# One transformer trunk on one core: all 2 KB tiles of SBUF at one place modulo 256, and another order of work at the start

## The chip, the core and the metric

The kernel runs on one core of one Trainium2 chip. The metric is the device time of one execution in microseconds (us); the time of the kernel before is the median of three runs. Differences under 0.2% (3.8 us here) can hardly be told from none.

TensorE (PE) multiplies matrices: a *stationary* tile of 128 by 128 is loaded (a row named PEld), and a *moving* tile of up to 512 columns is streamed past it. VectorE (DVE), ScalarE (ACT) and GpSimd (POOL) do the elementwise work, and SyncE (SP) issues the transfers from HBM to the on-chip memory SBUF, which has 128 partitions. A tile lies at one address in all partitions; "place modulo 512" is that address, in bytes, modulo 512.

## What is computed

Two layers on a sequence of 256 rows of 1024 numbers, all in float32. Cut to what matters here:

```
cond = silu(c)
for l in range(2):
    sh1, sc1, g1, sh2, sc2, g2 = split(cond @ w_ada[l] + b_ada[l], 6)
    h = rms_norm(x) * (1 + sc1) + sh1
    x = x + g1 * token_mixer(h, ... w_in[l], ..., w_branch_a/b/c[l], w_out[l])
    h = rms_norm(x) * (1 + sc2) + sh2
    f = swiglu(h, ffn_w_gate, ffn_w_up, ffn_w_down) if l == 0 else moe_ffn(h, router, 8 experts, top 2)
    x = x + g2 * f
return rms_norm(x, final_norm_w)
```

## The kernel before

Every weight comes from HBM once, in pieces of 1 MB (128 partitions of 8 KB, the tile `raw`), issued by SP as soon as a `raw` buffer is free. To keep float32 accuracy on TensorE each piece is split into a high part and the rest: ACT writes `whi` (L170) and DVE writes `wlo = raw - whi` (L172), and the activations are split in the same way (`hh` and `hl`, `ah` and `al`, `xx`, `act`, `yh` and `yl`). A product is then three matmuls, which `mm3` issues: high by high, high by low, low by high. All are recorded at L96, so that they are told apart by their tiles. In the rows a matmul reads as `out<-moving,stationary`, whichever operand is named first: where both are listed, the weights `whi` and `wlo` are the moving operand for `hh`, `hl`, `ah`, `al`, `act`, `xx`, `yh`, `yl`, and in the convolutions of the mixer (256 columns) it is the other way round.

The stages follow one another: the start (`start`, layer 0's modulation, its normalised input `x`, and the first four column blocks of `w_in`), the mixer of layer 0, the dense feed-forward block, the mixer of layer 1, and the mixture of experts (`moe`), which takes from 870 us to the end. In `moe` each expert multiplies its gathered rows `xx` (128 rows, 8 stationary tiles for the high and 8 for the low part, written by `gather`) with 28 pieces of gate and up weights, in 7 blocks of 4 pieces. A piece is 4 x 3 matmuls of 512 columns, a block 48 of them, and between two blocks stand the 4 transposes of the block before (L1566). Then 14 pieces of down weights are multiplied with `act`, 168 matmuls. There are 8 experts, so 56 blocks.

The order in the start is made by the order of the code and by a scheduler, which may move an instruction ahead of others on its engine. In a step `k` of the 8 steps there, DVE reduces two columns of the modulation (L199), ACT applies them to `xT` (L353), writes `hh` (L354) and the high parts of the weights (L347), and DVE writes the low parts (L357) and `hl` (L355). A group of matmuls on a high part alone (`warm`, 8 of them) keeps TensorE at work before the first step.

Tiles come from pools which lie one behind the other in SBUF, so that the place of every tile follows from the sizes of those ahead of it in its pool and in the pools before.

Of the kernel before, what the change touches and what calls it, by code (L numbers as in the profile page):

```python
# [10 lines left out]
F32 = mybir.dt.float32  # L11
# [3 lines left out]
AF = mybir.ActivationFunctionType  # L15
# [4 lines left out]
P = 128  # L20
D = 1024
S = 256
NT = S // P
# [38 lines left out]
def trunk_kernel(ctx, tc, a, out, dbg=None):  # L62
# [5 lines left out]
    wp = ctx.enter_context(tc.tile_pool(name="wp", bufs=2))  # L68
    pp = ctx.enter_context(tc.tile_pool(name="pp", bufs=2, space=PSUM))

    ones = cp.tile([P, P], F32, name="ones")
    V.memset(ones, 1.0)
    xs = cp.tile([P, NT, D], F32, name="xs")
# [1 line left out]
    pv = [cp.tile([P, NPP], F32, name=f"pv{l}") for l in range(DEPTH)]  # L75
    pos = cp.tile([P, NT], I32, name="pos")
    rt = cp.tile([P, KD, NE], F32, name="rt")
    ident = cst[:, C_ID:C_ID + P]
    U = cst[:, C_U:C_U + P]
    mask = cst[:, C_MASK:C_MASK + P]  # L80
# [24 lines left out]
    def small(w, name, dt=F32, bufs=2):  # L105
        return cp.tile([P, w], dt, name=name, tag=name, bufs=bufs)
# [38 lines left out]
    def load_raw(src, k, n, raw=None):  # L145

        raw = raw_tile() if raw is None else raw
        last["load"] = nc.sync.dma_start(raw[:, :k * n], src)
        return raw
# [161 lines left out]
    def start(tile, puts, ready):  # L311


        crow = [tile("crow") for _ in range(2)]
        for c in range(2):
            nc.sync.dma_start(crow[c][0:1, :], a["c"][:, c * 512:(c + 1) * 512])
        loads()
        for c in range(2):
            ps = smtile()
            mm(ps, ones[0:1, :], crow[c][0:1, :], True, True)  # L320
            A.activation(sc_b[:, c * 512:(c + 1) * 512], ps, AF.Silu)
        bias = pv[0][:, PP_BADA:PP_BADA + 48].rearrange("p (a b n) -> p a b n", a=2, b=3)[:, :, 1]
        V.tensor_scalar(bias, bias, 1.0, None, op0=OP.add)
        xn = [[tile("xn") for _ in range(2)] for _ in range(NT)]
        rs = start_scales(lambda t, c: xn[t][c])
        for t in range(NT):
            A.activation(xn[t][0], xs[:, t, :512], AF.Copy, scale=rs[t])
            V.tensor_scalar(xn[t][1], xs[:, t, 512:], rs[t], None, op0=OP.mult)
        xT = [tile("xT") for _ in range(4)]
        for i in range(4):  # L330
            ps = trtile()
            for j in range(2):
                for t in range(NT):
                    k = 2 * i + j
                    T.transpose(ps[:, j * S + t * P:j * S + (t + 1) * P], xn[t][k // 4][:, k % 4 * P:(k % 4 + 1) * P], ident)
            if i % 2:
                V.tensor_copy(xT[i], ps)
            else:
                A.activation(xT[i], ps, AF.Copy)
        acc = {}  # L340
        for k in range(KD):
            ra = load_raw(a["w_ada_pair"][0, 0, k], 1, 2 * D)
            rw = load_raw(a["w_first"][k], 1, 1872)
            parts = []
            for o, n in ((0, 848), (848, 1024)):
                hi, lo = ring()
                A.activation(hi[:, :n], rw[:, o:o + n], AF.Copy)  # L347
                parts.append((hi, lo, o, n))
            if k == 0:
                warm(parts[0][0], WARM)  # L350
            run(ada_cols(0, k, KD, ra))
            x = xT[k // 2][:, k % 2 * S:(k % 2 + 1) * S]
            A.activation(x, x, AF.Identity, scale=modc[0][:, 8 + k:9 + k], bias=modc[0][:, k:k + 1])  # L353
            last["copy"] = A.activation(hh[:, k], x, AF.Copy)  # L354
            last["sub"] = V.tensor_sub(hl[:, k], x, hh[:, k].bitcast(F32))  # L355
            for hi, lo, o, n in parts:
                V.tensor_sub(lo[:, :n], rw[:, o:o + n], hi[:, :n].bitcast(F32))  # L357
            if not acc:
                acc.update({(0, 0): mmtile(), (0, 1): mmtile(), (1, 0): mmtile(), (1, 1): mmtile(), (2, 0): smtile(),
                            (2, 1): smtile(), (3, 0): smtile(), (3, 1): sstile()})  # L360
            for first, (l_, r_) in enumerate(((hh, 0), (hl, 0), (hh, 1))):
                for t in range(NT):
                    for i, (c0, n) in enumerate(FIRST):
                        w = parts[i // 2]
                        mm(acc[i, t][:, :n], l_[:, k, t * P:(t + 1) * P], w[r_][:, c0 - w[2]:c0 - w[2] + n],
                           k == 0 and first == 0, k == KD - 1 and first == 2)
        ready()
        for i, (c0, n) in enumerate(FIRST):
            for t in range(NT):
                puts[i](t, acc[i, t][:, :n])  # L370
# [55 lines left out]
    def run(gen):  # L426
        for _ in gen:
            pass
# [104 lines left out]
    def mixer(l, after=None):  # L533

        with tc.tile_pool(name=f"mx{l}", bufs=1, reuse_waits="tile") as mp, \
                tc.tile_pool(name=f"mb{l}", bufs=1, reuse_waits="tile", side="right") as bp, \
                tc.tile_pool(name=f"mc{l}", bufs=1, reuse_waits="tile", side="right") as qp:

            def wg(name, dt=F32):
                return mp.tile([P, 512], dt, name=name, tag="w2k", bufs=16)  # L540
# [769 lines left out]
    def moe(l):  # L1310
        with tc.tile_pool(name=f"mw{l}", bufs=1, reuse_waits="tile", side="right") as xp, \
# [11 lines left out]
            sel = mp.tile([P, NT, NE], F32, name="sel")  # L1323
            ovi = mp.tile([P, 4], I32, name="ovi")
            ovs = mp.tile([P, 3, 2, NT], F32, name="ovs")
            with tc.tile_pool(name=f"mr{l}", bufs=1, reuse_waits="tile") as rp, \
                    tc.tile_pool(name=f"me{l}", bufs=1, reuse_waits="tile") as ep:
                rest, weights = route(l, rp, h2, slot, wsel, sel)
                pair = lambda e: choose(mp, [lambda t, i=i: slot[:, t, i:i + 1] for i in (e, e + 1)])
                Pm = pair(0)  # L1330
                behind("Pm", rest)
                ready = [(x, Pm, i) for i, x in enumerate(gather(l, ep, h2, Pm, 2, True))]
                behind("xl", weights)
                late = {16: 2, 17: 3, 27: 3}
                ahead.extend(load_raw(first_srcs[i], 4, 512, shot(xp, late[i], "raw") if i in late else None)
                             for i in range(15, 28))
                row_tile[l, 5] = lambda: mp.tile([P, 512], F32, name="g2", tag="g2", bufs=2)
                ada_rows(l, 5)
                g2 = [rows[l, 10 + c] for c in range(2)]

                def after_first(c):
                    if c == 1:
                        with tc.issue_after(last["act"].ins), tc.issue_after(last["tr"].ins):
                            overflow_data(ep, slot, wsel, sel, ovi, ovs)
                def finish():

                    fw, o, f = (raw_tile() for _ in range(3))
                    nc.sync.dma_start(fw[:, :D], a["final_w"])
                    o, f = (x.rearrange("p (t n) -> p t n", t=NT) for x in (o, f))
                    for t in range(NT):  # L1350
                        rs = rms_scale(t, lambda c: o[:, t, c * 512:(c + 1) * 512])
                        for c in range(2):
                            cs = slice(c * 512, (c + 1) * 512)
                            G.tensor_mul(f[:, t, cs], xs[:, t, cs], fw[:, cs])
                        for c in range(2):
                            cs = slice(c * 512, (c + 1) * 512)
                            if c:
                                V.tensor_scalar(o[:, t, cs], f[:, t, cs], rs, None, op0=OP.mult)
                            else:
                                A.activation(o[:, t, cs], f[:, t, cs], AF.Copy, scale=rs)  # L1360
                            nc.sync.dma_start(out[t * P:(t + 1) * P, cs], o[:, t, cs])

                for e in range(NE):
                    x, Pm, i = ready.pop(0)

                    def between():
                        Pm = behind("lo", pair, e + 1)
                        ready.extend((x, Pm, i) for i, x in enumerate(gather(l, ep, h2, Pm, 2)))
                    expert(l, e, ep, xp, x, lambda t, Pm=Pm, i=i: Pm[:, t, i], lambda t, e=e: wsel[:, t, e:e + 1], g2,
                           after_first if e == 0 else None, between if e % 2 and e < NE - 1 else None)  # L1370
                stages.flush()
                finish()
                overflow(l, mp, ep, xp, h2, g2, ovi, ovs, finish)
# [281 lines left out]
        for _ in range(n):  # L1655
            mm(ps, x[:, :P], x[:, :512], True, True)

    WARM = 8

    def late_loads():  # L1660
        with tc.issue_after(last["load"].ins):
# [5 lines left out]
            nc.sync.dma_start(rt.rearrange("p k n -> p (k n)"), a["moe_router"][0, 0, 0])  # L1667

    def loads():
        for t in range(NT):  # L1670
            nc.sync.dma_start(xs[:, t], a["x"][t * P:(t + 1) * P])
        nc.sync.dma_start(cst[:, :C_U], a["consts"][:, :C_U])
        nc.sync.dma_start(pv[0], a["params"][0])

# [121 lines left out]
```

## Time and profile before

| | |
|---|---|
| median of 3 runs | 1892.44 us (1891.72 to 1893.65) |
| the profiled execution | 1891.01 us, of which the span from first to last instruction is 1889.2 us |
| PE busy | 97% of the span, 9490 matmuls |
| DVE busy | 85% |
| ACT busy | 65% |
| HBM read | 527.41 MB, 280 GB/s over the span |
| chain that ended last | PE 87%, DVE 6%, ACT 3% |

The profile is of one execution. A matmul's row has its start and a duration that overlaps the next one, so the distance from one start to the next, here called a step, says how fast TensorE goes, and the duration does not. The chain that ended last is followed back from the last instruction, at each point to what released it. Its pieces of TensorE run from the first start of a group to the next group, so that a piece of n matmuls divided by n is the mean step.

### The profile page before, as it was taken

How to read it: one execution, taken by the hardware profiler on the slowest of the kernel's cores; microseconds unless marked ns; L12 is line 12 of the kernel's file. 1: busy time of each engine (PE TensorE's matmuls, PEld its weight loads, DVE VectorE, ACT ScalarE, POOL GpSimd, SP SyncE). 2: the span in 40 equal slices, each digit the busy share in tenths (PEclk: the TensorE clock that was granted, in tenths of full speed). 3: DMA queues.
4: the chain of work that ended last, by engine and by line, in shares of the span. 5: the costliest groups of instructions: out<-in, count | busy, mean ns of one | idle time of the engine just before them, and what ended most of it. 6: DMA issues, size and time to landing. Idle time of an engine off the chain costs nothing.

```text
span 1889.2 us, 25651 instructions
## 1 busy us (share of the span) xinstructions
PE 1841.5 (97%) x9490; PEld 1545.4 (82%) x9490; DVE 1602.2 (85%) x2313; ACT 1231.6 (65%) x1599; POOL 43.3 (2%) x61
## 2 busy tenths in 40 slices
PE   8999999999999999999999999999999999999996
PEld 6899887788889998888887878878778888788785
DVE  7998788777578978877999989998898999899997
ACT  4665445644466644457777777777877777777775
POOL 0000010000000000100000000000000000000001
PEclk9999999999999999999999999999999999999998
DMA  9453457677644654758998989999899999899892
GB/s 365 160 202 131 171 198 270 235 257 263 211 144 148 221 184 173 276 204 357 340 354 331 356 313 362 363 359 349 331 352 344 354 363 367 307 357 378 336 353 84
DMA packets 75016, 530.19 MB, mean 281 GB/s; under 512 B 8578, under 2 KB 8962, under 8 KB 12548
## 3 DMA queue, kind: packets, MB, share of 16 engines
q1 hardware_dynamic: 74884, 528.49, 74.1%
q8 instruction: 76, 1.25, 0.3%
q14 instruction: 56, 0.46, 0.1%
HBM read 527.41 MB, written 1.05 MB: 280 GB/s over the span
## 4 chain that ended last, share of the span: by engine, by line
PE 87%; DVE 6%; ACT 3%; issue 2%; DMA 2%; DVEq 0%; ACTq 0%; SPq 0%
PE mmt L96 76%; PE smt L96 6%; DVE wlo L172 2%; PE sst L96 2%; PE trt L1566 1%; DVE raw L199 1%; ACT whi L170 1%; PE trt L258 1%; ACT sg L1527 1%; DMA raw<-in_ffn_w_down_dram 0%; PE trt L1073 0%; PE trt L96 0%; DMA raw<-in_w_ada_pair_dram 0%; DMA raw<-in_w_out_dram 0%; DMA raw<-in_w_ada_gate_dram 0%
## 5 line engine op out<-in xcount | busy, mean ns | idle before, releaser
L172 DVE TENSOR_TENSOR wlo<-raw,whi 128x1024 fp32r<-128x1024 f32 (+1 forms) x874 | 1043.7, 1223 | 128.1 <-ACT whi L170 107.1
L170 ACT ACTIVATE whi<-raw 128x1024 fp32r<-128x1024 f32 (+1 forms) x874 | 908.2, 1059 | 305.2 <-PE mmt L96 253.4
L96 PE MATMUL mmt<-whi,xx 128*128 128x512 f32 x1792 | 579.0, 398 | 0.0
L96 PEld LDWEIGHTS mmt<-whi,xx 128*128 128x128 f32 x1792 | 337.4, 188 | 75.0
L96 PE MATMUL mmt<-wlo,xx 128*128 128x512 f32 x896 | 357.6, 399 | 4.9 <-DVE wlo L172 4.9
L96 PE MATMUL mmt<-whi,act 128*128 128x512 f32 x896 | 281.0, 391 | 1.2 <-ACT whi L170 1.2
L96 PEld LDWEIGHTS mmt<-wlo,xx 128*128 128x128 f32 x896 | 168.8, 188 | 52.3 <-DVE wlo L172 16.4
L96 PEld LDWEIGHTS mmt<-whi,act 128*128 128x128 f32 x896 | 167.5, 188 | 36.4 <-ACT whi L170 2.5
L96 PE MATMUL mmt<-whi,hh 128*128 128x512 f32 (+2 forms) x480 | 184.0, 389 | 5.8 <-ACT hh L292 2.0
L96 PE MATMUL mmt<-whi,hl 128*128 128x512 f32 (+2 forms) x480 | 181.1, 383 | 0.5 <-DVE hl L293 0.5
L96 PE MATMUL mmt<-wlo,hh 128*128 128x512 f32 (+2 forms) x480 | 181.2, 383 | 0.0
L96 PE MATMUL mmt<-wlo,act 128*128 128x512 f32 x448 | 175.3, 391 | 1.8 <-DVE wlo L172 1.6
L199 DVE CUSTOM_DVE_ANT_0 raw<-raw,sc_b,pv 128x1024 f32<-128x1024 f32 x96 | 123.2, 1298 | 12.8 <-DMA raw<-in_w_ada_pair_dram 9.8
L96 PEld LDWEIGHTS mmt<-whi,hh 128*128 128x128 f32 x480 | 91.0, 190 | 23.7 <-ACT hh L292 2.6
L96 PEld LDWEIGHTS mmt<-whi,hl 128*128 128x128 f32 x480 | 90.7, 189 | 18.0 <-DVE hl L293 1.0
L96 PEld LDWEIGHTS mmt<-wlo,hh 128*128 128x128 f32 x480 | 90.9, 189 | 16.2 <-DVE wlo L172 0.2
L96 PEld LDWEIGHTS mmt<-wlo,act 128*128 128x128 f32 x448 | 84.1, 188 | 22.3 <-DVE wlo L172 4.4
L96 PE MATMUL mmt<-hh,whi 128*128 128x256 f32 x320 | 92.3, 290 | 0.5 <-ACT whi L170 0.5
L96 PE MATMUL mmt<-hh,wlo 128*128 128x256 f32 x320 | 90.6, 287 | 1.1 <-DVE wlo L172 1.1
L96 PE MATMUL mmt<-hl,whi 128*128 128x256 f32 x320 | 91.0, 285 | 0.0
L1549 ACT ACTIVATE act<-trt 128x512 fp32r<-128x512 f32 x56 | 33.1, 591 | 72.0 <-PE trt L1566 72.0
L1549 DVE TENSOR_TENSOR act<-trt,act 128x512 fp32r<-128x512 f32 x56 | 38.6, 689 | 33.2 <-ACT act L1549 32.7
(422 smaller groups left out, 2226.9 us busy)
## 6 DMA issues: line engine op xcount, KB each, us to landing
raw<-in_moe_w_gate_dram SPq DMA_DIRECT2D x112, 1024.0 KB, 6.0
raw<-in_moe_w_up_dram SPq DMA_DIRECT2D x112, 1024.0 KB, 6.2
raw<-in_moe_w_down_dram SPq DMA_DIRECT2D x112, 1024.0 KB, 6.9
raw<-in_w_in_dram SPq DMA_DIRECT2D x50, 1024.0 KB, 4.9
raw<-in_w_ada_pair_dram SPq DMA_DIRECT2D x32, 1024.0 KB, 5.0
raw<-in_w_ada_gate_dram SPq DMA_DIRECT2D x16, 1024.0 KB, 4.9
raw<-in_ffn_w_down_dram SPq DMA_DIRECT2D x11, 1024.0 KB, 5.5
raw<-in_ffn_w_gate_dram SPq DMA_DIRECT2D x10, 1024.0 KB, 4.9
```

The source lines that it names most:

```text
L96: return T.matmul(o, l, r, start=start, stop=stop, skip_group_check=True)
L170: last["hi"] = A.activation(hi[:, :m], r, AF.Copy)
L172: last["lo"] = V.tensor_sub(lo[:, :m], r, hi[:, :m].bitcast(F32))
L199: last["ada"] = V.tensor_tensor_reduce(r, r, sc_b, 1.0, pv[l][:, PP_BADA + i:PP_BADA + i + 1], OP.mult, OP.add, modc[l][:, i:i + 1])
L258: T.transpose(ps[:, j * S + t * P:j * S + (t + 1) * P], src(t, b0 + j), ident)
L1527: A.activation(tmp[:, o], ps[:, o], AF.Identity, scale=sc, bias=sh)
L1549: return trace(*args, **kw)
L1566: last["tr"] = T.transpose(ps[:, b * P:(b + 1) * P], sg[:, b * P:(b + 1) * P], ident)
```

## The change

**Layout.** A helper `gap(pool, n)` allocates an unused tile of n bytes a partition. Six such gaps (192 bytes in the pool of constants, 128 in the mixer's, 224 in `mo`, 160 and 32 in `me` of the experts) move what lies behind them. No instruction comes with a gap. By the two built programs, tiles that TensorE reads begin at these places modulo 512; tiles longer than 2 KB are cut in slices at multiples of 512 bytes, so the place holds for each slice:

| tile, stage | role | before | after |
|---|---|---|---|
| `whi`, `wlo`, all stages | moving | 480 | 224 |
| `hh`, `hl`, start, mixers, dense gate and up | stationary | 480 | 224 |
| `ah`, `al`, dense down | stationary | 480 | 480 |
| `yh`, `yl`, mixers | stationary | 480 | 480 |
| `act`, experts' down | stationary | 480 | 480 |
| `xx`, experts' gate and up | stationary | 96 | 224 |
| `ohi`, `olo`, `qhi`, `qlo`, mixers | moving | 96 | 480 |
| `Pm`, gather of the experts | moving | 256 | 224 |

Modulo 256, 480 and 224 are the same place, 224.

**Start.** The first half of `x` is transferred ahead of the two halves of `c`; a small activation loads Silu's table early; `WARM` goes from 8 to 3; all transposed pieces `xT` are copied out of PSUM by ACT, three of them after `hh` of step 0; and in step 0 the second high part follows these copies. From step 2 on the instructions and their waits are those of before on every engine but for three waits named otherwise.

```diff
+    def gap(pool, n):
+
+        pool.tile([P, n // 4], F32, name="gap", tag=f"gap{n}")
+
...
+    gap(cp, 192)
...
+        A.activation(small(1, "silu0"), ones[:, :1], AF.Silu)
         crow = [tile("crow") for _ in range(2)]
+        nc.sync.dma_start(xs[:, 0], a["x"][:P])
         for c in range(2):
             nc.sync.dma_start(crow[c][0:1, :], a["c"][:, c * 512:(c + 1) * 512])
         loads()
...
-            if i % 2:
-                V.tensor_copy(xT[i], ps)
-            else:
-                A.activation(xT[i], ps, AF.Copy)
+            return ps
+        pst = [turned(i) for i in range(3)]
+        A.activation(xT[0], pst[0], AF.Copy)
...
+            run(ada_cols(0, k, KD, ra))
+            if k:
+                high(0, 848)
+                high(848, 1024)
+                hidden()
+            else:
+                high(0, 848)
                 warm(parts[0][0], WARM)
...
+                behind("hi", hidden)
+                pst.append(turned(3))
+                for i in range(1, 4):
+                    behind("copy", A.activation, xT[i], pst[i], AF.Copy)
+                behind("copy", high, 848, 1024)
...
+            gap(mp, 128)
...
+            gap(mp, 224)
...
+                gap(ep, 160)
...
+                            gap(ep, 32)
...
-    WARM = 8
+    WARM = 3
...
-        for t in range(NT):
-            nc.sync.dma_start(xs[:, t], a["x"][t * P:(t + 1) * P])
+        nc.sync.dma_start(xs[:, 1], a["x"][P:])
```

What `behind(name, f, ...)` does: f's instructions are placed no earlier than the last instruction that was recorded under that name.

SP's queue at the very beginning, before the change (`crow` is c, `xs` is x, `cst` and `pv` are constants, `raw` a piece of weights):

```order
L316 DMA crow<-in_c_dram 1x512 x2
L1671 DMA xs<-in_x_dram 128x1024 x2
L1672 DMA cst<-in_consts_dram 128x128
L1673 DMA pv_68<-in_params_dram 128x175
L148 DMA raw<-in_w_ada_pair_dram 128x2048
```

The same place of SP's queue after the change:

```order
L321 DMA xs<-in_x_dram 128x1024
L323 DMA crow<-in_c_dram 1x512 x2
L1696 DMA xs<-in_x_dram 128x1024
L1697 DMA cst<-in_consts_dram 128x128
L1698 DMA pv_68<-in_params_dram 128x175
L153 DMA raw<-in_w_ada_pair_dram 128x2048
```

One transfer of x now stands ahead of the two of c.

ACT's queue from its first work to the high parts of step 0, before the change (`xn,ss` is the sum of squares, `sc_b` is silu(c), `xT` the transposed input, `modc` the modulation; an ACTIVATE from `trt` to `xT` copies a transposed piece out of PSUM; names in brackets are the semaphores waited for):

```order
L321 ACTIVATE sc_b<-smt 128x512 [waits PE_49] x2
L299 ACTIVATE xn,ss_121<-xs 128x512 [waits DMAHW2_49]
L299 ACTIVATE xn,ss_121<-xs 128x512 [waits DMAHW3_49]
L327 ACTIVATE xn<-xs,rs_129 128x512 [waits DVE_49,Activation_49]
L327 ACTIVATE xn<-xs,rs_129 128x512 [waits Activation_49]
L339 ACTIVATE xT<-trt 128x512 [waits PE_49]
L353 ACTIVATE xT<-xT,modc_78 128x256 [waits DVE_49,Activation_49]
L339 ACTIVATE xT<-trt 128x512 [waits PE_49]
L347 ACTIVATE whi<-raw 128x848 [waits DMAHW7_49]
L347 ACTIVATE whi<-raw 128x1024
L354 ACTIVATE hh<-xT 128x256 [waits Activation_49]
```

The same place of ACT's queue after the change:

```order
L304 ACTIVATE xn,ss_125<-xs 128x512 [waits DMAHW3_49]
L328 ACTIVATE sc_b<-smt 128x512 [waits PE_49] x2
L334 ACTIVATE xn<-xs,rs_133 128x512 [waits DVE_49,Activation_49]
L334 ACTIVATE xn<-xs,rs_133 128x512 [waits Activation_49]
L346 ACTIVATE xT<-trt 128x512 [waits PE_49]
L356 ACTIVATE whi<-raw 128x848 [waits DMAHW7_49]
L360 ACTIVATE xT<-xT,modc_79 128x256 [waits DVE_49,Activation_49]
L361 ACTIVATE hh<-xT 128x256 [waits Activation_49]
L1575 ACTIVATE xT<-trt 128x512 [waits PE_49]
L1575 ACTIVATE xT<-trt 128x512
L1575 ACTIVATE xT<-trt 128x512 [waits PE_49]
L356 ACTIVATE whi<-raw 128x1024
```

The two activations for `sc_b` moved behind the sums of squares, `hh` of step 0 moved ahead of three copies to `xT`, and the second `whi` of step 0 moved behind them.

DVE's queue from the normalised input to the first reduction of step 1, before the change (`wlo` and `hl` are the low parts; an ISA row with `raw,modc` is a reduction of L199, and the short one behind it reads its sum):

```order
L328 TENSOR_SCALAR xn<-xs,rs_129 128x512 [waits DVE_49]
L328 TENSOR_SCALAR xn<-xs,rs_129 128x512
L199 ISA raw,modc_78<-raw,sc_b,pv_68 128x1024 [waits DMAHW6_49]
L199 ISA modc_78 128x1
L199 ISA raw,modc_78<-raw,sc_b,pv_68 128x1024
L199 ISA modc_78 128x1
L337 COPY xT<-trt 128x512 [waits PE_49] x2
L357 TENSOR_TENSOR wlo<-raw,whi 128x848 [waits DMAHW7_49,Activation_49]
L357 TENSOR_TENSOR wlo<-raw,whi 128x1024 [waits Activation_49]
L355 TENSOR_TENSOR hl<-xT,hh 128x256 [waits Activation_49]
L199 ISA raw,modc_78<-raw,sc_b,pv_68 128x1024 [waits DMAHW0_49]
```

The same place of DVE's queue after the change:

```order
L335 TENSOR_SCALAR xn<-xs,rs_133 128x512 [waits DVE_49]
L335 TENSOR_SCALAR xn<-xs,rs_133 128x512
L204 ISA raw,modc_79<-raw,sc_b,pv_68 128x1024 [waits DMAHW6_49,Activation_49]
L204 ISA modc_79 128x1
L204 ISA raw,modc_79<-raw,sc_b,pv_68 128x1024
L204 ISA modc_79 128x1
L377 TENSOR_TENSOR wlo<-raw,whi 128x848 [waits DMAHW7_49,Activation_49]
L362 TENSOR_TENSOR hl<-xT,hh 128x256 [waits Activation_49]
L204 ISA raw,modc_79<-raw,sc_b,pv_68 128x1024 [waits DMAHW0_49]
L204 ISA modc_79 128x1
L377 TENSOR_TENSOR wlo<-raw,whi 128x1024 [waits Activation_49]
```

The copies to `xT` left DVE, and the second `wlo` of step 0 moved behind `hl` and the first reduction of step 1.

## Rows read from the trace of the kernel before

**Rows 1.** The page, busy time: us, share of the span, instructions.

```profile
PE 1841.5 (97%) x9490; PEld 1545.4 (82%) x9490; DVE 1602.2 (85%) x2313; ACT 1231.6 (65%) x1599; POOL 43.3 (2%) x61
...
PE 87%; DVE 6%; ACT 3%; issue 2%; DMA 2%; DVEq 0%; ACTq 0%; SPq 0%
```

**Rows 2.** Chain that ended last, experts: start us, us, what.

```profile
1390.66 11.16 PE mmt L96 x48
1401.82 0.44 PE trt L1566 x4
1402.26 11.17 PE mmt L96 x48
...
1425.50 11.31 PE mmt L96 x48
...
1460.57 38.56 PE mmt L96 x169
```

**Rows 3.** The same chain, dense gate and up, dense down, mixer 1.

```profile
365.16 21.12 PE mmt L96 x93
...
472.20 55.60 PE mmt L96 x245
...
765.45 58.28 PE mmt L96 x257
```

**Rows 4.** Timeline of TensorE, experts' gate and up: start us, us, instruction.

```profile
1401.66 0.60 PE L1566 MATMUL trt<-cst,sg 128*128 128x128 f32 x4
1402.02 0.48 PE L96 MATMUL mmt<-whi,xx 128*128 128x512 f32 x1
1402.33 0.40 PE L96 MATMUL mmt<-wlo,xx 128*128 128x512 f32 x1
...
1405.13 0.39 PE L96 MATMUL mmt<-wlo,xx 128*128 128x512 f32 x1
...
1407.92 0.39 PE L96 MATMUL mmt<-wlo,xx 128*128 128x512 f32 x1
```

**Rows 5.** Timeline of TensorE, the beginning of the dense down product.

```profile
472.27 0.40 PE L96 MATMUL mmt<-whi,al 128*128 128x512 f32 x1
...
474.12 0.39 PE L96 MATMUL mmt<-wlo,ah 128*128 128x512 f32 x1
...
475.93 0.39 PE L96 MATMUL mmt<-whi,ah 128*128 128x512 f32 x1
```

**Rows 6.** Timeline of TensorE, output product of mixer 1.

```profile
835.78 0.40 PE L96 MATMUL mmt<-ohi,hh 128*128 128x512 f32 x1
...
838.58 0.40 PE L96 MATMUL mmt<-ohi,hh 128*128 128x512 f32 x1
```

**Rows 7.** Windows: stretch, length, busy of PE, PEld, DVE, ACT, POOL; PEclk, DMA share, GB/s.

```profile
1207.86:1246.00 38.14, 38.14 (x170) 31.41 (x169) 34.95 (x32) 31.36 (x32) 0.00 (x0) 1.00 0.98 391
...
1514.18:1584.20 70.02, 70.02 (x313) 56.24 (x313) 63.57 (x61) 52.77 (x59) 0.00 (x0) 1.00 0.93 361
```

**Rows 8.** Groups of DVE's instructions in the experts: xcount | busy us, mean ns.

```profile
L1549 DVE TENSOR_TENSOR act<-trt,act 128x512 fp32r<-128x512 f32 x56 | 38.6, 689 | 33.2 <-ACT act L1549 32.7
...
L1533 DVE TENSOR_TENSOR xx<-sg,xx 128x512 fp32r<-128x512 f32 x16 | 11.0, 689 | 6.1 <-ACT xx L1532 6.1
```

**Rows 9.** Timeline of the start, ACT and DVE and two rows of TensorE.

```profile
6.57 0.69 DVE L300 CUSTOM_DVE_ANT_0 xn<-xs 128x512 f32<-128x512 f32 x1 [0.60 <-DMA xs<-in_x_dram]
...
7.35 0.62 ACT L299 ACTIVATE xn<-xs 128x512 f32<-128x512 f32 x1
...
8.09 0.17 DVE L303 TENSOR_SCALAR ssd<-ss 128x2 f32<-128x2 f32 x1 [0.74 <-ACT xn L299]
...
15.19 0.69 DVE L337 COPY xT<-trt 128x512 f32<-128x512 f32 x1 [0.85 <-PE trt L335]
...
15.79 3.78 PE L96 MATMUL sst<-whi 128*128 128x512 f32 x8 [0.63 <-ACT whi L347]
...
17.16 1.86 ACT L347 ACTIVATE whi<-raw 128x848 fp32r<-128x848 f32 x2 [0.17 <-DMA raw<-in_w_first_dram]
...
23.06 1.27 DVE L199 CUSTOM_DVE_ANT_0 raw<-raw,sc_b,pv 128x1024 f32<-128x1024 f32 x1
...
29.45 1.28 DVE L199 CUSTOM_DVE_ANT_0 raw<-raw,sc_b,pv 128x1024 f32<-128x1024 f32 x1
...
45.92 0.65 PE L96 MATMUL mmt<-whi,hh 128*128 128x336 f32 x2 [0.68 <-ACT hh L354]
```

More of the change, by code (lines that the diff above doesn't have):

```diff
@@ L329, in start, with turned @@
         xT = [tile("xT") for _ in range(4)]
-        for i in range(4):
+        def turned(i):
             ps = trtile()
@@ L343, in start, with high, hidden @@
             rw = load_raw(a["w_first"][k], 1, 1872)
+            x = xT[k // 2][:, k % 2 * S:(k % 2 + 1) * S]
             parts = []
-            for o, n in ((0, 848), (848, 1024)):
+            def high(o, n):
                 hi, lo = ring()
-                A.activation(hi[:, :n], rw[:, o:o + n], AF.Copy)
+                last["hi"] = A.activation(hi[:, :n], rw[:, o:o + n], AF.Copy)
                 parts.append((hi, lo, o, n))
-            if k == 0:
-                warm(parts[0][0], WARM)
[L351 to L355, printed above, removed]
+            def hidden():
+                A.activation(x, x, AF.Identity, scale=modc[0][:, 8 + k:9 + k], bias=modc[0][:, k:k + 1])
+                last["copy"] = A.activation(hh[:, k], x, AF.Copy)
+                last["sub"] = V.tensor_sub(hl[:, k], x, hh[:, k].bitcast(F32))
+            run(ada_cols(0, k, KD, ra))
[5 more added lines that the diff above has]
+                high(0, 848)
+                warm(parts[0][0], WARM)
+                behind("hi", hidden)
[3 more added lines that the diff above has]
+                behind("copy", high, 848, 1024)
             for hi, lo, o, n in parts:
```

## The prediction

> **What bounds the kernel now.** I read the page first. TensorE is busy 97% of the span and makes 87% of the chain that ended last, DVE 6%, ACT 3% [rows 1]. So the time is the sum of TensorE's steps plus what it waits for, and the question is which steps the change makes shorter.
>
> The second view is the chain, piece by piece, divided by the number of matmuls. In the dense gate and up product 21.12 us / 93 = 227.1 ns, in the dense down product 55.60 / 245 = 226.9, in mixer 1 58.28 / 257 = 226.8 [rows 3]. In the experts' down product it is 38.56 / 169 = 228.2, but in their gate and up blocks 11.16 to 11.31 us / 48 = 232.5 to 235.6 [rows 2]. All of these are matmuls of 512 columns with the same moving tiles `whi` and `wlo`, on the same engine.
>
> The third view, the timeline, shows that this is no stall here and there. Inside a gate and up block 12 steps in a row take 1407.92 - 1405.13 = 2.79 us, 232.5 ns each [rows 4], and this goes on to the end of the block. The dense down product also begins like that: 8 steps in 474.12 - 472.27 = 1.85 us, 231 ns each; but the next 8 take 1.81 us, 226.3 each, and it stays there [rows 5]. So there is a fast rhythm of 226 to 227 ns that most products fall into after some 8 steps, and that the gate and up blocks never find.
>
> What sets these blocks apart is not that they are gate and up products (the dense ones are fast), nor that they belong to the experts (their down product is fast under the same traffic). It is the place of the stationary tile: `xx` begins at 96 modulo 512, the moving tiles at 480; in all fast products both stand at 480. A second place bears this out from the other side: in the output product of mixer 1 the stationary tile is the usual `hh`, at 480, but the moving tiles `ohi` and `olo` stand at 96, and 12 steps take 838.58 - 835.78 = 2.80 us, 233.3 each [rows 6]. So either operand displaced by 128 modulo 256 keeps the fast rhythm away. The trace shows the coincidence in several products; it does not show the mechanism.
>
> **The change, part by part.** *The experts' gate and up blocks.* After the change `xx` and the moving tiles both stand at 224. If equal places modulo 256 are what counts, each block settles into 226.8 ns [rows 3], but only after some 8 steps at 231, 8 x 4.4 = 35 ns, after each break. One break a block is certain (the transposes: the step behind them is 1402.33 - 1402.02 = 0.31 us [rows 4]); as pieces differ by up to 0.15 us [rows 2], I take two. A block saves 48 x (232.5 - 226.8) = 274 ns, less 70, so 204 ns, and 56 blocks save 11.4 us. Bounds: nothing lost at breaks 15.3 us, three breaks 9.4 us.
>
> Does another engine take over? In a stretch of gate and up blocks of 70.02 us DVE is busy 63.57 us and ACT 52.77 [rows 7]; the stretch would shrink by about 1.2 us, and DVE then has 5 us to spare. Transfers run at 361 GB/s there and would need 367; the down product of an earlier expert ran at 391 for 38 us [rows 7]. So both covers hold; if one of them gave out, the loss would be at most the gain itself.
>
> *The output and latent products.* 96 matmuls move `ohi`, `olo`, `qhi` or `qlo`; at 233.3 against some 228 that is 0.5 us, below by 0, above by 96 x 6.5 = 0.6.
>
> *Other tiles that move.* DVE writes `xx` at 96 in 689 ns and `act` at 480 in 689 ns [rows 8], so the elementwise work does not see its place; zero, and DVE's spare time hides a few ns anyway. Matmuls of 256 columns or fewer I leave at zero as well, within 0.4 us either way (some 128 of them, in the gather, with 3 ns each, half of the difference of places seen above).
>
> *The start.* ACT takes its second sum of squares at 7.35, behind the two `sc_b`, although the second half of x had landed by 6.57; its sum is what DVE waits 0.74 us for until 8.09 [rows 9]. With `sc_b` behind it, that sum comes about 0.7 us earlier: 6.57 + 0.62 + the read of the sum, 7.4. `sc_b` itself is first needed some 3 us later. From there the work of steps 0 and 1 passes through DVE and ACT in turn until the first reduction of step 2 at 23.06; from then on each step is as before (29.45 - 23.06 = 6.39 us [rows 9]). DVE loses two copies of 0.69 us and the 0.85 us wait ahead of the second [rows 9], but gains a wait: the second `wlo` of step 0 now follows three copies and a high part on ACT. Placing the rows' durations one behind the other in the new order, I get the reduction of step 2 at 22.0, 1.0 us earlier. Bounds: 0, because step 1's weights land at 17.16 as before and ACT waits for them [rows 9]; and 2.1, the 0.7 plus the two copies. Behind that reduction stand only steps that keep their order, so the gain carries to the end. The five `warm` matmuls dropped, 3.78 x 5/8 = 2.4 us [rows 9], cost and save nothing: TensorE does not wait between the steps until 45.92, when it has caught up and waits 0.68 us for ACT's `hh` [rows 9]. If that cover is gone, that is if TensorE stayed at the warm group's 0.47 us a matmul through some 24 matmuls of step 0, it would lose 24 x 0.24 = 6 us, less the 2.4, and still catch up: each later step leaves it about 1 us, as that wait and the step of 6.39 us show.
>
> **Sum.** 11.4 + 0.5 + 1.0 = 12.9 us. The profiled execution took 1891.01 us, 1.8 more than its span and 1.4 under the median, so it would become 1878.1, and the median of the kernel 1892.44 - 12.9 = 1879.5 us. With the bounds, 9.4 + 0 + 0 - 0.4 to 15.3 + 0.6 + 2.1 + 0.4, this case reaches from 1874.0 to 1883.4.
>
> **The rivals.** *The place counts modulo 512.* The program before cannot tell 256 from 512, since every fast pair stands at 480 and 480. After the change the moving tiles stand at 224 and `act`, `ah`, `yh` stay at 480. Then gate and up blocks gain 11.4 and the others lose the rhythm: 8 x 168 with `act`, 240 in the dense down, 288 with `yh` and `yl`, 64 with `ah` as the moving tile, 1936 in all, x 5.7 ns = 11.0, less some 0.8 that they pay at breaks now: 10.2. Net 11.4 + 1.0 - 10.2 = 2.2, so 1890.2 us. For it: nothing in the rows speaks against it. Against it: the only displacement that the rows show to be slow, 128, is covered by the smaller rule.
>
> *The layout does nothing.* Something that only goes along with `xx` and `ohi` would make them slow, and the gain is the start's 1.0 us: 1891.4 us. Against it: the two products have nothing else in common [rows 4, 6], and the gate and up blocks lie between fast down products of the same expert [rows 2]. The Trainium skill speaks for this rival: "SBUF — State Buffer", section "Who interferes with whom", has the matmul's moving operand and the weight load on two independent read ports of TensorE, and says that TensorE never waits on anyone; by that no place of a tile could slow a step. The rows above do not agree with this (226.3 against 232.5 and 233.3).
>
> *The place itself counts, modulo 512.* If the rhythm needs the moving tile at 480 and not just two equal places, the ring's move to 224 takes it from every product, and gate and up gain nothing. The loss is the 1936 above and 1320 matmuls with `hh` and `hl` in the start, the mixers and the dense block, 3256 x 5.7 = 18.6, less some 2 at breaks, less the start's 1.0: 1892.4 + 15.6 = 1908 us, slower. It decides from the first settled product on: dense gate and up at 232 instead of 227.1. Against it: a rule that prefers 480 to 224 modulo 512 would be odd beside products that care for a shift of either operand; the rows cannot exclude it.
>
> **How the numbers follow.** Equal places modulo 256 count: 0.70. Modulo 512: 0.14. Nothing: 0.09. The absolute place: 0.05. The rest, 0.02, is for a start or an engine that I have misread. The likeliest case gives 1879.5 us, own range 1874 to 1883.5. For 8 in 10 the range must take in the modulo 512 case, so 1874 to 1890.5. A measurement of this kernel tells a difference from none from about 0.2% on, 3.8 us. The first case is faster by more than that; the second, at 2.2 us, falls there 2 times in 10 and else within; the third within; the fourth slower. Faster 0.73, same 0.21, slower 0.06.
>
> **What would show it.** In the chain of the changed kernel the gate and up pieces of 48 should fall from 11.16-11.31 to about 11.0 us, while the pieces of 93, 245, 257 and 169 stay; in the timeline the blocks should settle at 226 to 227 ns and the output product too. If instead down and dense down rise to 232, it is modulo 512; the output product then stays at 233, since `ohi` at 480 meets `hh` at 224. If all of them rise, it is the place itself. The first reduction of step 2 should start near 22.0. I am wrong in size if DVE's waits grow in the blocks, so that steps settle but pieces do not shrink.

## The result

The changed kernel takes 1880.14 us (median of 4 runs, 1879.30 to 1881.75), the kernel before 1893.05 in the same runs: a ratio of 0.9935, 95% interval 0.9922 to 0.9949. Predicted were 1879.5 us. A second measurement gave 1879.35 us and 0.9933 (0.9921 to 0.9945). The profiled execution took 1879.70 us, its span is 1877.9; the profile before had 1891.01 and 1889.2, so the two traces account for 11.3 us.

The busy times of the changed kernel's page (us, share, instructions) answer to [rows 1]: TensorE is busy 13.7 us less, some 2.4 of them by the five `warm` matmuls that are gone (3.78 x 5/8, [rows 9]), and its share of the span is what it was.

```profile
PE 1827.8 (97%) x9485; PEld 1540.8 (82%) x9485; DVE 1599.4 (85%) x2311; ACT 1233.1 (66%) x1602; POOL 42.9 (2%) x61
```

The chain that ended last, with the pieces that answer to [rows 2, 3]: dense gate and up, dense down, mixer 1, an experts' down product, and gate and up blocks.

```profile
365.24 21.13 PE mmt L101 x93
...
472.09 55.59 PE mmt L101 x245
...
765.06 58.28 PE mmt L101 x257
...
1203.13 38.41 PE mmt L101 x169
...
1384.45 10.93 PE mmt L101 x48
...
1430.16 11.17 PE mmt L101 x48
```

The dense products and mixer 1 stand within 0.01 us of before, the down product gained 0.15 us, and the gate and up blocks fell from 11.16 to 10.93 us, or from 11.31 to 11.17. (The pieces of 11.16 and 10.93 have one break, those of 11.31 and 11.17 two.) This alone decides against two rivals: `act`, `ah` and `yh` stand at 480 modulo 512 and their moving tiles at 224, yet 38.41 / 169 = 227.3 ns, so the place does not count modulo 512, nor must it be 480.

The timeline of TensorE inside a block, for [rows 4]:

```profile
1395.23 0.60 PE L1592 MATMUL trt<-cst,sg 128*128 128x128 f32 x4
1395.89 0.40 PE L101 MATMUL mmt<-wlo,xx 128*128 128x512 f32 x1
...
1398.65 0.39 PE L101 MATMUL mmt<-wlo,xx 128*128 128x512 f32 x1
...
1401.37 0.39 PE L101 MATMUL mmt<-wlo,xx 128*128 128x512 f32 x1
```

A `wlo` row comes every third step. From 1395.89 to 1398.65 12 steps take 2.76 us, 230 ns each; the next 12 take 2.72 us, 226.7 each. The fast rhythm is there, and it is found some 10 steps behind the transposes. The output product of mixer 1, for [rows 6], now has it too: 12 steps in 2.72 us.

```profile
835.35 0.39 PE L101 MATMUL mmt<-ohi,hh 128*128 128x512 f32 x1
...
838.07 0.39 PE L101 MATMUL mmt<-ohi,hh 128*128 128x512 f32 x1
```

A stretch of gate and up blocks, for [rows 7]: DVE and the transfers keep pace as forecast (364 GB/s, 367 expected; DVE spare 5.6 us).

```profile
1506.60:1575.67 69.07, 69.07 (x313) 56.12 (x313) 63.51 (x61) 52.72 (x59) 0.00 (x0) 1.00 0.94 364
```

The timeline of the start and one wait further on, for [rows 9]:

```profile
6.78 0.69 DVE L305 CUSTOM_DVE_ANT_0 xn<-xs 128x512 f32<-128x512 f32 x1 [1.74 <-DMA xs<-in_x_dram]
...
17.73 1.23 DVE L377 TENSOR_TENSOR wlo<-raw,whi 128x1024 fp32r<-128x1024 f32 x1 [0.76 <-ACT whi L356]
...
22.50 1.28 DVE L204 CUSTOM_DVE_ANT_0 raw<-raw,sc_b,pv 128x1024 f32<-128x1024 f32 x1
...
115.32 0.63 PE L834 MATMUL trt<-cst,sc 128*128 128x128 f32 x4 [0.83 <-DVE sc L828]
```

The first row is the work on x's second half, the last but one the first reduction of step 2. It came 0.56 us earlier than before, not 1.0; and at 115 us TensorE waits 0.83 us for DVE's softmax in mixer 0, a wait that the profile of before does not have.

### The profile page after: what moved, and what is told of

The parts are those of the page before. It is cut to its first block, busy times and chain, and to the rows that moved or that the text cites. A ratio compares the mean times of both kernels' runs of the same rounds, so it can differ in the third digit from the quotient of the medians.

```text
span 1877.9 us, 25643 instructions
## 1 busy us (share of the span) xinstructions
PE 1827.8 (97%) x9485; PEld 1540.8 (82%) x9485; DVE 1599.4 (85%) x2311; ACT 1233.1 (66%) x1602; POOL 42.9 (2%) x61
## 4 chain that ended last, share of the span: by engine, by line
PE 83%; DVE 8%; ACT 4%; DMA 2%; issue 2%; SPq 0%; DVEq 0%; ACTq 0%
PE mmt L101 73%; PE smt L101 5%; DVE wlo L177 2%; DVE raw L204 1%; PE trt L1592 1%; PE sst L101 1%; DMA raw<-in_w_ada_gate_dram 1%; ACT whi L175 1%; DVE cv L610 1%; ACT sg L1553 1%; DMA raw<-in_w_in_dram 1%; PE trt L263 1%; PE trt L1095 0%; ACT whi L356 0%; PE trt L101 0%
## 5 line engine op out<-in xcount | busy, mean ns | idle before, releaser
L101 PE MATMUL mmt<-whi,xx 128*128 128x512 f32 x1792 | 571.6, 393 | 0.0
```

What stands on the lines that cost most here:

```text
L101: return T.matmul(o, l, r, start=start, stop=stop, skip_group_check=True)
```

## The experiments

**The two parts apart.** First the six gaps with the old start, and the new start without any gap (all gap lines taken out).

> The six gaps alone, with the start of the kernel before. If the places make the gain: the experts shorten by some 10.5 us, as in the changed kernel, the mean step of their gate and up products falls from 232.9 to 228.9 ns, and the time is 1893.0 - 12.3 = 1880.7 us; the first reduction of step 2 in the start stays near 23.06. If the gain is not from the places but from the other start: about 1893 us, step 232.9.

Measured: 1889.11 us, ratio 0.9981 (0.9971 to 0.9990). Gate and up are as fast as in the changed kernel, but the chain shows dense down and the experts' down slow:

```profile
364.66 21.11 PE mmt L101 x93
...
471.69 57.07 PE mmt L101 x245
...
886.87 10.92 PE mmt L101 x48
...
1206.77 39.27 PE mmt L101 x169
```

> The new start alone, without the gaps. If the places make the gain: the first reduction of step 2 starts near 22.5 us, all later stages are those of before, gate and up step at 232.9 ns, and the time is some 0.6 us below before, 1892.4 us, a ratio of 0.9997 that times can hardly show. If the start had a hidden part in it: nearer to 1880 us. The changed kernel lost 0.8 us between 96 and 161 us; if the start makes that, it is seen here too, otherwise it belongs to the layout.

Measured: 1895.14 us, ratio 1.0021 (1.0011 to 1.0030), 2.7 us slower than forecast.

Neither agreed with any theory as I had written it, and the two effects did not add up to that of the change. The cause is in the places of the built programs. The new start has a one-column tile (`small(1, "silu0")`), and with its two buffers it takes 64 bytes of the pool of constants; all pools behind that one are displaced by 64, while `act`, `ah` and `yh`, whose pools are laid from the other end of SBUF (`side="right"`), stay. Without the small tile the ring (the buffers of `whi` and `wlo`) stands at 160 and `act` still at 480: 192 apart modulo 256 (ring less stationary), and the mean step of `act` is 233.3 ns. With it and no gaps the ring stands at 32, so 64 apart, and the step is 229.2. So the small tile is a part of the layout change, which the diff lists under the start. The two runs were a test of the rule by accident: the same instructions behind the start, another relation, another step.

The parts once more, with every tile in its right place:

```diff
-    gap(cp, 192)
+    gap(cp, 256)      (old start, all six gaps)
...
+    gap(cp, 192)      (new start, no other gap)
```

> The gaps alone, the first one 64 bytes longer, because the one-column tile of the new start, which is missing here, takes 64 bytes of the pool of constants: so every tile stands where it stands in the changed kernel. If the relation modulo 256 makes the gain: act against the ring back from 233.3 to 227.4 ns, gate and up at 228.3 or less, the experts some 10.5 us shorter, 1892.4 - 11.6 = 1880.8 us. If the layout without the new start is not enough: about 1889 us, as with the shorter gap.

Measured: 1881.06 us, ratio 0.9950 (0.9936 to 0.9963). `act` steps at 227.3 ns, `xx` at 228.9 as in the changed kernel, and a down product takes 38.41 us again:

```profile
882.97 10.93 PE mmt L101 x48
...
1201.10 38.41 PE mmt L101 x169
```

> The new start with one gap of 192 bytes, which with the 64 bytes of the small tile makes 256, so that every relation between moving and stationary tiles is that of the kernel before (xx 128 apart, the others equal). If the relation is all that layout does: gate and up at 232.9 to 233.1 ns, act at 227.3, and the start's own gain, 0.75 us from the landing of x's second half to the first reduction of step 2 (15.72 us later instead of 16.49), so 1891.7 us, a ratio of 0.9996. If the start had a loss of its own behind the layout's: near 1895 us, as without the gap.

Measured: 1892.65 us, ratio 1.0001 (0.9990 to 1.0012); `xx` at 232.9, `act` at 227.2. The layout makes the gain; what the start brings is below what can be measured.

**A relation, or a place?**

```diff
-    gap(cp, 192)
+    gap(cp, 64)
...
+    gap(hp_, 128)
     hh = hp_.tile([P, KD, S], F32R, name="hh")
```

> The changed kernel with the ring of whi and wlo, and everything in the experts that lies behind it, displaced by 128 to 96 modulo 256; hh, hl, ah, act, yh stay at 224. If the relation between moving and stationary tile counts: gate and up, now 96 with 96, keep a mean step of 228.9 ns; act, dense gate, up and down, the first products of the mixers, 224 against 96, rise from 227.4 to about 232.7; some 3250 matmuls of 512 columns x 5.1 ns = 16.6 us, so 1897 us. If a tile at 96 is slow by itself: gate and up return to 232.9 as well, and the time is near 1907 us. If only xx at 96 is slow, whatever the moving tile: 1891 us, and the products with act and hh stay at 227.4.

Measured: 1891.40 us, ratio 0.9997 (0.9988 to 1.0007). The chain:

```profile
365.22 21.61 PE mmt L102 x93
...
473.07 56.85 PE mmt L102 x245
...
768.75 59.73 PE mmt L102 x257
...
890.39 10.91 PE mmt L102 x48
...
1210.17 39.14 PE mmt L102 x169
```

Now `xx` and the ring share 96, the place at which `xx` was slow before, and gate and up are fast; all else, 128 apart, is slow (232.4, 232.0, 232.4 and 231.6 ns a step). It is the relation of the two operands. The total rose by 12 us and not by 16.6. The unbroken steps that slowed are some 3000, not 3250, and those with `hh` and `hl`, the mixers' short runs among them, stood at 228.4 before they rose to 232.4; by their means the slowed steps lost some 14 us, and `xx` gained 1.4 (228.3 against 228.9 ns).

**How far apart.** Each expert's `xx` gets a place of its own; the high and low parts of a pair are then written by two instructions in place of one.

```diff
-        xx = ep.tile([P, 2, 2, KD, P], F32R, name="xx", tag="xx")
+        xf = ep.tile([P, 4152], F32R, name="xx", tag="xx")
+        d = 16 * (nth[0] % 4)
+        nth[0] += 1
+        xx = [xf[:, d + 2056 * e:d + 2056 * e + 2 * KD * P]... for e in range(2)]
```

> The changed kernel with xx at another place for each expert: relative to the ring 192, 160, 128, 96, 64, 32, 0 and 224 bytes modulo 256, for experts 0 to 7. If only equal places are fast: one expert (the seventh) steps at 228.9 ns, the others at 232.9, and the time is 1880 + 7/8 x 10.5 = 1889 us. If only the half in which a tile lies counts (displacement of 128): some four experts are fast and four slow, 1885 us. If nothing but exactly 128 is slow: one slow expert, 1881.5 us. If the loss grows with the distance: steps between 228.9 and 232.9 in order of distance.

Measured: 1890.37 us, a single execution. Blocks without a second break, one from each of experts 0 to 7 (rows of the chain):

```profile
885.53 11.20 PE mmt L101 x48
...
1008.71 11.24 PE mmt L101 x48
...
1138.61 11.16 PE mmt L101 x48
...
1262.00 11.20 PE mmt L101 x48
...
1391.71 11.00 PE mmt L101 x48
...
1514.28 11.21 PE mmt L101 x48
...
1643.79 10.93 PE mmt L101 x48
...
1766.08 11.20 PE mmt L101 x48
```

With the displacement as place of the moving tile less that of the stationary one: 192, 160, 128, 96, 64, 32, 0, 224. By these rows the mean step is 227.8 ns at 0, 229.2 at 64 (229.2 also in the run without gaps), and 232.5 to 234.2 elsewhere; once settled it is 226.7, 228.9, and 232.4 to 234.3. So "equal or not" held but for the one value between, 64, and the loss does not grow with the distance.

**By itself.** Behind the end of the changed kernel, with all else idle, series of 48 matmuls; a stationary tile `st` and a moving one `mv`, displaced by the number of bytes that the series is named after.

```diff
+        def series(name, ds, n=48, cols=512, dm=0):
+            ps = pp.tile([P, 512], F32, name=name, tag="mm", bufs=4)
+            for i in range(n):
+                d = ds[i % len(ds)] // 4
+                mm(ps[:, :cols], st[:, d + P * (i % 8):d + P * (i % 8 + 1)],
+                   mv[:, dm // 4 + 512 * (i % 2):][:, :cols], i == 0, i == n - 1)
```

> The changed kernel with 25 series of 48 matmuls behind its end, when DVE, ACT and the transfers are done: a stationary tile at 0 to 256 bytes from the place of the moving one, then other column counts. If the relation acts between TensorE's own two reads: with all other engines idle the series settle as in the experts, 226.7 at 0 and 256, 229 at 64, 232 to 234 at 32, 96, 128, 160, 192, 224, and moving the other tile gives the same with the sign turned. If the loss needs the writes of other engines or of transfers: all series settle at 226.7. Finer displacements, 4 to 16: no forecast beyond that they lie between. If the loss comes from the load of 128 columns against the stream, 384 and 256 columns show it too, in ns about as large a step.

The window over all series (columns as in [rows 7]) shows the other engines and the transfers idle:

```profile
1885.00:2168.00 283.00, 283.00 (x1345) 237.90 (x1343) 0.00 (x0) 0.00 (x0) 0.00 (x0) 1.00 0.00 1
```

In TensorE's timeline each series is a row; from its start to that of the next one, divided by 48, is its mean step.

```profile
1929.16 11.05 PE L101 MATMUL zero<-mv,st 128*128 128x512 f32 x48
1940.05 11.32 PE L101 MATMUL four<-mv,st 128*128 128x512 f32 x48
1951.21 11.23 PE L101 MATMUL eight<-mv,st 128*128 128x512 f32 x48
1962.28 11.36 PE L101 MATMUL sixteen<-mv,st 128*128 128x512 f32 x48
...
2018.30 11.32 PE L101 MATMUL half<-mv,st 128*128 128x512 f32 x48
2029.45 11.37 PE L101 MATMUL hundredsixty<-mv,st 128*128 128x512 f32 x48
2040.65 11.16 PE L101 MATMUL threequarters<-mv,st 128*128 128x512 f32 x48
2051.65 11.36 PE L101 MATMUL last<-mv,st 128*128 128x512 f32 x48
2062.85 11.04 PE L101 MATMUL full<-mv,st 128*128 128x512 f32 x48
2073.73 11.17 PE L101 MATMUL movingquarter<-mv,st 128*128 128x512 f32 x48
2084.73 11.35 PE L101 MATMUL movingthree<-mv,st 128*128 128x512 f32 x48
...
2107.06 11.05 PE L101 MATMUL bothhalf<-mv,st 128*128 128x512 f32 x48
2117.94 11.35 PE L101 MATMUL alternating<-mv,st 128*128 128x512 f32 x48
```

Equal places: (1940.05 - 1929.16) / 48 = 226.9 ns, 226.7 with `st` displaced by a full 256 bytes, 226.7 with both displaced by 128. Unequal: 232.5 at 4 bytes, 230.6 at 8, 232.3 at 128. The value between of the sweep is here at `st` displaced by 192, 229.2, and at `mv` by 64, 229.2. That is the displacement of the sweep, +64 counted from the stationary tile. My forecast had put it at `st` displaced by 64, the wrong sign (there it is 233.3). The 230.6 at 8 bytes is a second value between. With `st` displaced by 0 and 128 in turn from one matmul to the next the settled step is 233.3, no better than displaced throughout. So no write of another engine and no transfer is needed: the loss lies between TensorE's two operands. The Trainium skill, "SBUF — State Buffer", section "Who interferes with whom", has two independent read ports for them; these rows do not show them as independent of each other's place, and the measurement decides. Which part of the path makes the loss, no run here tells.

At 384 columns the settled step is 173.3 ns equal and 176.0 at 128; at 256 columns 120.0 and 118.7, the other way round; at 128 columns 111.7 both. So the price of 6 ns belongs to 512 columns and does not carry to shorter matmuls, as far as this one displacement and one profile show it.

**The rest of the loss in a block.** In the changed kernel 22 of the 47 gate and up pieces of 48 in the chain take 10.93 to 10.97 us, 25 take 11.13 to 11.17. In the longer ones the second piece of weights begins late: two steps take 292 and 341 ns, and the rhythm is to be found again. The step-by-step timeline has the same late start in the same 25 blocks before the change, there with two steps of 264 and 339 ns on the mean. ACT's timeline shows why the high parts are late, first of the kernel before, then of the changed one:

```profile
1043.67 0.60 ACT L1549 ACTIVATE act<-trt 128x512 fp32r<-128x512 f32 x1 [2.16 <-PE trt L1566]
```

```profile
1040.59 0.60 ACT L1575 ACTIVATE act<-trt 128x512 fp32r<-128x512 f32 x1 [2.10 <-PE trt L1592]
1041.08 2.00 ACT L175 ACTIVATE whi<-raw 128x1024 fp32r<-128x1024 f32 x2
```

The copy of `act` stands in ACT's queue and waits 2.16 or 2.10 us for the transposes; the high parts behind it wait too.

```diff
-            yield 1
+            yield 2
             if c % 2 == 0:
                 act.append(shot(xp, c // 2, "act", F32R))
```

> The changed kernel with the copy and the low part of act one piece of weights later, so that ACT, which waits 2.1 us for the transposes in each block, takes the next high part first. In 21 of 56 blocks of the changed kernel the second piece begins late (292 and 341 ns instead of two steps of 227) and the rhythm is lost again for some 9 steps. If ACT's place in its queue makes that second break: 21 x 0.23 = 4.8 us less than the changed kernel, 1875.5 us. If the ring of whi and wlo makes it: no change, or a few us more because the transposed tile's PSUM buffer is held longer.

Measured: 1874.49 us, ratio 0.9911 (0.9896 to 0.9926). In the chain all 47 such pieces take 10.93 or 10.94 us, so the order in ACT's queue made the second break; ACT's wait for the transposes is gone:

```profile
1040.74 1.06 ACT L175 ACTIVATE whi<-raw 128x1024 fp32r<-128x1024 f32 x1 [0.30 <-PE mmt L101]
1041.71 0.58 ACT L1575 ACTIVATE act<-trt 128x512 fp32r<-128x512 f32 x1
```

**The changed kernel again, and a filled wait.**

> The changed kernel once more, unchanged, for its difference to the layout alone and to the later copy of act. If the start is worth some 0.5 us: a ratio to before near that of the layout alone, 0.995 less 0.0003, about 1881 us. If layout and start together bring more than each alone (0.9935 against 0.995 and 1.0001): again 0.9935.

Measured: 1879.35 us, ratio 0.9933 (0.9921 to 0.9945). The interval overlaps with that of the layout alone, so the difference of 1.7 us between the two is not shown.

```diff
+                    if i == 4:
+                        pw, x = sstile(), parts["s", 0][0][0]
+                        with tc.issue_after(last["hT"].ins):
+                            for _ in range(12):
+                                mm(pw[:, :336], x[:, :P], x, True, True)
                     step(*job)
```

> The kernel with the later copy of act, and 12 matmuls without use, 336 columns each, in the 2.0 us in which TensorE waits for hh at the start of mixer 1. In most profiles TensorE's granted clock is at its lower level for some 3.4 us right after that wait; in the profile of the layout alone it is not, and there the stretch up to the 3000th matmul was 2.3 us shorter. If the wait is what lets the clock fall: full clock throughout, some 2 us less, 1872.5 us. If something else does: no change, 1874.5, or up to 0.2 us more because the 12 matmuls end after hh is there.

Measured: 1872.52 us, ratio 0.9895 (0.9882 to 0.9908), the fastest version here. The third figure from the right in a window's row is the granted clock. The window behind the wait in the changed kernel:

```profile
540.00:545.00 5.00, 2.98 (x12) 2.67 (x12) 2.03 (x4) 4.98 (x13) 0.00 (x0) 0.77 0.18 75
```

The same window in the profile of its second measurement:

```profile
540.00:545.00 5.00, 3.00 (x17) 2.76 (x18) 2.14 (x4) 4.98 (x13) 0.00 (x0) 1.00 0.14 57
```

And with the wait filled:

```profile
540.00:545.00 5.00, 4.68 (x30) 4.07 (x29) 1.51 (x3) 4.80 (x12) 0.00 (x0) 1.00 0.27 115
```

With the wait filled the clock stayed at its upper level. But it did so in the second profile of the changed kernel too, with the same wait of 2.03 us, so one profile proves nothing on what keeps it there. What a fall costs can be read: from the end of the wait to the hundredth matmul behind it the first profile of the changed kernel takes 18.36 us, the second 16.83, so 1.5 us. The times speak for some 2 us by the filled wait, with intervals that overlap; whether the filling is what kept the clock stays open.

## Why the prediction was right, step by step

**The rhythm and its cause.** Right: the relation modulo 256 of the two operands sets it. The rows of before could only show that 0 was fast and 128 slow; the sweep and the series alone fill in the rest. Of the rivals, modulo 512 and the absolute place fell with the profile after and with the displaced ring, "the layout does nothing" with the two parts apart.

**The size, gate and up.** Forecast 11.4 us. The mean of the unbroken `xx` steps fell from 232.89 to 228.91 ns, on 2500 steps 9.95 us; with the broken steps all `xx` matmuls together are 10.3 us shorter. Where a block has one break the forecast holds: 274 - 35 = 239 ns by its terms, and 240 measured (11.256 us from the first matmul to the transposes before, 11.016 after, the mean of 21 blocks). The break itself costs some 50 ns and not 35 (10.93 us against 48 x 226.67 ns = 10.88), but a settled step also gains more than 5.7 ns. The term that was mis-sized is the second break, which I had put at another 35 ns in every block: 25 of the 47 blocks have it, the same ones before and after, and they gained 145 ns and not 204 (11.385 to 11.240 us, the mean of 18 of them). So a second break costs 0.22 us now where it cost 0.13: with a faster TensorE the two steps around it last some 632 ns where they lasted 603, and behind it the fast rhythm is to be found again, which these blocks did not have before. A part of the gain thus went into a wait for ACT that had been there all along, while the forecast had looked at ACT's busy time and not at the order in its queue. With the later copy of `act` all `xx` matmuls together are another 5.7 us shorter; by the times it is 4 to 5 us (1879.35 - 1874.49 = 4.9, each measured beside other runs of the kernel before). The 4.8 that were forecast for it had counted 21 blocks, so that they agree is partly luck.

**Covers.** Right: DVE and the transfers did not become the bound (5.6 us of DVE spare in the stretch of [rows 7], 364 GB/s).

**Output and latent products.** Forecast 0.5 us; of the 96 steps with these tiles the 92 unbroken ones fell from 232.5 to 227.9 ns, 0.4 us.

**The start.** Too large. From x's second half in SBUF to the first reduction of step 2 it was 23.06 - 6.57 = 16.49 us before, and 16.36 to 16.42 in the two other profiles with the old start; with the new one it is 15.71 to 15.74 in seven of nine (16.07 and 16.14 in the others). So the new order gains 0.7 us; I had placed the reduction 22.0 - 6.57 = 15.4 us behind, a gain of 1.1. DVE's waits for `whi`, 1.20 us ahead of the first `wlo` and 0.76 ahead of the second at 17.73, are in that; the forecast had no number for either, so which of them it had too small can't be told. And x's second half landed at 6.78, and between 5.83 and 6.97 in the other profiles with the new start (6.34 to 6.57 with the old), which eats a part. And "the gain carries to the end" failed: ahead of the wait of 0.83 us in mixer 0 TensorE's matmuls are 0.57 us earlier than before, behind it 0.30 later. That wait is 0 to 1.29 us from profile to profile, with either start, so I can't lay it to the change.

**The sum.** 12.9 us forecast, 11.3 by the two profiles, 12.9 by the medians. By the start times of the same matmuls in both profiles, 10.5 of the 11.3 us arise in the experts, behind 870 us. The fall of the clock at 542 us is in both profiles and has no part in it. That the medians agree so well with the forecast is partly luck: gate and up gave 1.1 to 1.5 us less and the start next to nothing, and the changed kernel's medians move by a microsecond from one measurement to the next.

**Warm matmuls.** Dropping five cost nothing that the profile shows: TensorE starts step 0 at 15.34, where it was 19.37, steps at 0.23 us for 512 columns from 18.55 on, and waits for ACT at 21.30 already.

## What to carry to other kernels

When a matmul's step stands a few per cent above that of another one with the same shape, compare the addresses of both operands before looking for a stall: no wait is shown, only the distance from start to start. Check the relation again after every edit that allocates anything, however small, since 64 bytes more or less for a tile of one column decided over some 6 us (ratios 0.9981 and 0.9950). And when the bound engine gets faster, look again at the breaks that it had all along: they cost more now, here 0.22 us for 0.13, and one instruction in ACT's queue that nobody needed yet made 25 of them.

## What was not expected of the hardware

- The step of 512 columns depends on the operands' places to within 4 bytes: 226.7 ns at 0 and 256 bytes, 232.5 at 4, 230.6 at 8, 229.2 where the moving tile stands 64 above the stationary one, else 232 to 234.4, with TensorE alone at work.
- With equal places the rhythm takes some 10 steps to settle behind the transposes (233, 236, 224, 231, 236, 228, 233, 231 and then 226, 227, 227), 39 ns more than settled steps by this list, some 50 for the whole break.
- Steps settle into a pattern that repeats to the nanosecond or two, for instance 226, 229, 232 with the moving tile 64 above the stationary one and 234, 233, 233 at 192; a displacement can have two (at 192 also 231, 236).
- TensorE's granted clock was at its lower level (1.2 GHz) for some 3.4 us at the end of a wait of 2.0 us near 542 us in 8 of 12 profiles (6.8 us in one of them), and not in three others with the same wait; 336 columns then took 280 ns a step and not 153, and the fall cost 1.5 us.
